# First norm by scale and transpose, decay matrices from running sums by transfer, and a refitted schedule table in a hybrid RG-LRU / DeltaNet layer

## Chip, cores and metric

One core of a Trainium2 chip runs the whole program. The metric is the device time of one execution in microseconds (us); three runs of the kernel before took 1097.16, 1097.39 and 1097.98 us, so the median is 1097.39 us.

## What is computed

One encoder layer on 512 tokens of 1024 features, all in float32: a norm, one wide projection, two token mixers side by side, a gated merge, a second norm and a SwiGLU. Cut to what matters here:

```
h = rmsnorm(x, mix_norm);  p = h @ w_in                      # 512 x 9248
y_rnn = rglru_branch(...)  @ w_rnn_proj                      # sigmoid, tanh, exp, sqrt, gelu; scans in both directions
y_dn  = deltanet_branch(...) @ w_dn_proj                     # 8 heads, both directions
x = x + (sig(g1) * y_rnn + sig(g2) * y_dn) @ w_out
x = x + (silu(h2 @ wg) * (h2 @ wu)) @ w_down;  h2 = rmsnorm(x);  out = rmsnorm(x)
# inside deltanet_branch, per head, direction and chunk:
gc = cumsum(g);  decay[i, j] = exp(gc[i] - gc[j]) where i >= j, else 0
A = strict_lower((beta k) k^T * decay);  att = q k^T * decay;  solve (I + A) ...;  state passes from chunk to chunk
```

The decay matrix is what one edit of the change computes in another way. The kernel uses chunks of 128 tokens, so there are 4 chunks (`NT`), 8 heads and 2 directions: 64 decay blocks of 128x128, held as 16 tiles of 128x512.

## The kernel before

**Products.** Nearly all matmuls are made of fp32r parts: a float32 operand is cast to fp32r (`whi`, `hh`: a CAST on ACT) and the rest is kept as a second part (`wlo`, `hl`: a subtraction on DVE), and three products of the parts are added up in PSUM. So each weight block of 128 columns costs a transfer on SP's queue (`wraw`), a CAST of 128x1024 on ACT, a subtraction of 128x1024 on DVE and 24 matmuls with 512 moving columns on PE. `whi` and `wlo` have two buffers each, `wraw` three.

**Stages.** (1) The first norm: each 128-token chunk of x is loaded, its squares are summed (ACT for even chunks, DVE for odd ones), and `norm_transpose` (L490) brings it to feature-major form; it multiplies each 128x128 block of x by `dg`, a diagonal matrix of 1/rms, so one float32 matmul scales and transposes at once. (2) The RG-LRU branch in four groups of three blocks (`rg_front`, `rg_mid`, `rg_out`): projections, four gate products per block, then Sigmoid, Tanh, Exp, Sqrt and Gelu on ACT, which need different function tables (each change is one ACT_TABLE_LOAD), and scans on DVE. (3) The DeltaNet branch in four groups of two heads: `dn_front` (projections, SiLU, norms), `dn_mats` (L813: decay, A and att, written to the tile `na`), `dn_inverse`, `dn_state`, `dn_out`. Projections of other stages fill PE in between. (4) Output projection, second norm, then the feed-forward part, in which PE never pauses.

**The decay before.** For each head and direction `dn_mats` builds on DVE two fp32r tiles of 128x512, a triangular mask (`upi` or `loi`) times the high and the low part of g (`gh`, `gl`); two matmuls with a strict triangular matrix (`slr` or `sur`) add these up to gc[i] - gc[j] in PSUM (`pd`); ACT takes one Exp of 128x512; then GpSimd (POOL) sets the masked half to zero with `affine_select`. The products with k and q follow on DVE (`na`).

**The order of the work.** Every operation is recorded by `Rec` (L322), all with the same source line, L374. `Plan.order` (L147) then plays the program through on estimated costs and due times, and the instructions are issued in the order that comes out. A due time is an entry of the table `TIMES` (L36), one per call of `spend()`, plus an offset within the stage; entries past the table's end follow its largest. Each engine takes the ready operation that is due first; a tile is handed out only when its pool has room. So the table sets the order on every engine, and each engine's queue is then in order: an instruction that waits holds back all that stand behind it on its engine.

Of the kernel before, what the change touches and what calls it, by code (L numbers as in the profile page):

```python
# [32 lines left out]
RELEASE = 200  # L33
SLACK = {"ACT": 1.1, "DVE": 1.1, "POOL": 1.2}
LOOK = 40
TIMES = [  # L36
# [18 lines left out]
class Plan:  # L55

# [5 lines left out]
    LAG = {("PE", "PE"): 0, ("PE", "DVE"): 250, ("PE", "ACT"): 250, ("DVE", "PE"): 320, ("ACT", "PE"): 320, ("POOL", "PE"): 320,  # L62
           ("DVE", "DVE"): 130, ("DVE", "ACT"): 250, ("ACT", "ACT"): 50, ("ACT", "DVE"): 200, ("DVE", "POOL"): 250,
           ("POOL", "DVE"): 150, ("ACT", "POOL"): 250, ("SP", "SP"): 0}

    def __init__(self, nc):
        self.nc = nc
        self.ops = []
        self.where, self.bases = [], []
        self.t = self.base = 0.0  # L70
# [7 lines left out]
        self.fixed = 13.3  # L78
# [40 lines left out]
    def add(self, eng, fn, outs, ins, cost, tail=0.0, table=None):  # L119
# [22 lines left out]
        cost *= SLACK.get(eng, 1.0)  # L142
        self.ops.append((eng, fn, deps, touched, round(cost), round(1.25 * tail), table, self.t))
# [3 lines left out]
    def order(self):  # L147
# [13 lines left out]
        for i, o in enumerate(ops):  # L161
            for d in o[2]:
                users[d].append(i)
        uses, first, last = {}, {}, {}
# [7 lines left out]
        need = [sorted((x for x in o[3] if x in self.tile_tag), key=first.get) for o in ops]  # L172
        free = dict(self.tags)
        queue = {tag: [] for tag in self.tags}
        for name, key in first.items():
            queue[self.tile_tag[name]].append((key, name))
# [9 lines left out]
        pe_end, cold = 0, WARM  # L186
        result, start = [], {}

        def slots(i):
            want = [x for x in need[i] if x not in held]  # L190
            taken = {}
            for name in want:
# [8 lines left out]
                for key, other in queue[tag]:  # L201
# [38 lines left out]
        while True:  # L240
            for e in ENGINES:
# [7 lines left out]
                for name in want:  # L249
                    tag = self.tile_tag[name]  # L250
                    free[tag] -= 1
                    held.add(name)
                    inuse[tag].add(name)
                    queue[tag].remove((first[name], name))
                c = o[4]
                if e == "ACT" and o[6] is not None and table not in o[6]:
                    table = o[6][0]
                    c += 1283
                if e == "PE":
                    if now - pe_end > 3000:  # L260
                        cold = 0
                    if cold < WARM:
                        c *= 2
                        cold += c
                    pe_end = now + c
                end = done = now + c
# [18 lines left out]
            while events and events[0][0] == now:  # L285
                _, kind, i = heapq.heappop(events)
                o = ops[i]
                if kind == 0:
                    busy[o[0]] = False
                elif kind == 1:  # L290
# [4 lines left out]
                    for u in users[i]:  # L295
                        left[u] -= 1
                        if not left[u]:
                            wait = 0 if o[5] else self.LAG.get((o[0], ops[u][0]), 200)
# [23 lines left out]
class Rec:  # L322
# [5 lines left out]
    def __getattr__(self, op):  # L328
        real = getattr(self.real, op)

        def call(*a, **kw):
# [9 lines left out]
            table, tail = None, 0.0  # L341
            e = self.eng
            if op == "dma_start":
                tail = max(out.nbytes() / 360.0, 1)
                cost = 450 if e == "SP" else 1000 if e == "POOL" else 60
            elif e == "PE":
                rhs = a[2] if op == "matmul" else a[1]
                n = elems(out)
                four_ = rhs.dtype == F32
                cols = elems(a[1]) if op == "matmul" else P  # L350
                if op == "transpose" and self.plan.fixed > 3:
                    cost = 110
                elif four_:
                    cost = 33 if cols == 32 else 81 if cols == 64 else n * 4 / 2.4
                else:
                    cost = max(n / 2.4, 107 if rhs.dtype == F32R else 54) + (self.plan.fixed if rhs.dtype == F32R else 2.5)
            elif e == "ACT":
                cost = (51 if psum else 93) + 0.834 * n + 93 * (ptr if n > 1 else len(ins) - 1) + (93 if len(outs) > 1 else 0)
                if op == "activation":
                    table = Plan.TABLES.get(a[2])  # L360
            elif e == "DVE":
                if op == "reciprocal":
                    cost = 69 + 6.25 * n
                elif op in ("tensor_tensor", "tensor_tensor_scan"):
                    cost = 69 + 1.042 * n
                elif op == "scalar_tensor_tensor":
                    cost = 130 + 1.042 * n + (70 if len(outs) > 1 else 0)
                elif op == "transpose":
                    cost = 68 + 1.042 * n
                else:  # L370
                    cost = 68 + (1.042 if psum else 0.521) * n + 61 * ptr
            else:
                cost = {"tensor_tensor": 150 + 2.1 * n, "memset": 35 + 0.834 * n, "affine_select": 140 + 0.886 * n}.get(op, 240 + 0.84 * n)
            self.plan.add(e, lambda: real(*a, **kw), outs, ins, cost, tail, table)  # L374
# [5 lines left out]
def trunk(ctx: ExitStack, tc: tile.TileContext, x, mix_norm, w_in, rg_conv_w, rg_conv_b, rg_wa, rg_ba, rg_wx, rg_bx,  # L380
# [15 lines left out]
    ps = ctx.enter_context(tc.tile_pool(name="ps", bufs=3, space=PSUM))  # L396

# [51 lines left out]
    slr, sur = (const([P, P], n, F32R) for n in ("slr", "sur"))  # L449
# [9 lines left out]
    V.tensor_copy(slr, sl)  # L459
    V.tensor_copy(sur, su)  # L460
# [29 lines left out]
    def norm_transpose(srcs, dgs, gain_, hh, hl, c0):  # L490
# [14 lines left out]
    xs = []  # L505
    for c in range(NT):
        xc = four(shape=(P, D))
        Q.dma_start(xc, x[0, c * P:(c + 1) * P, :])
        xs.append(xc)
        if c == 1:  # L510
            plan.t = -20.0
    plan.t = -300.0
    gain = load_gain(mix_norm[0], "gain1")
    hh = new(hp, (P, KD, S), "hh", 1, F32R)
    hl = new(hp, (P, KD, S), "hl", 1, F32R)
    for c0 in (0, 2):
        norm_transpose(xs[c0:c0 + 2], [norm_scale(xs[c0 + i], i) for i in range(2)], gain, hh, hl, c0)
        plan.t = -15.0
    plan.t = 0.0
# [147 lines left out]
    gh, gl = const([P, 64], "gh", F32R), const([P, 64], "gl", F32R)  # L667
    V.tensor_copy(gh, gt)
    V.tensor_tensor(gl, gt, f(gh), ALU.subtract)
# [7 lines left out]
    egc, elast, egl = ge[:, 0, :], ge[:, 1, :], ge[:, 2, :]  # L677
    negc = const([P, 64], "negc")
# [773 lines left out]
```

## Time and profile before

| | |
|---|---|
| median of three runs | 1097.39 us (1097.16 to 1097.98) |
| span of the profiled execution, first to last instruction | 1095.2 us |
| between that span and the median | 2.2 us |
| PE busy | 1070.3 us, 6916 records |
| DVE busy | 826.6 us |
| ACT busy | 626.6 us, 77.0 of it table loads |
| POOL busy | 46.1 us |
| moved by DMA | 98.40 MB, 90 GB/s on average |

The time of the profiled execution itself is not recorded beside its span; the 2.2 us is what the median of the runs has above it. PE is the matmul engine; PEld, its weight loads, runs beside it. A busy figure counts an instruction from its start to its end; matmuls overlap, so a row's mean is longer than the time from one start to the next. "Idle before <- releaser" is the time that the engine stood still ahead of a group and who ended that. Since nearly all work has the line L374, groups are told apart by tiles: `t` is any work tile of the two general pools, `mm`, `ax` and `st` are PSUM banks.

### The profile page before, as it was taken

To read this page: it belongs to the slowest core of one execution; us is meant where nothing else is said; L and a number is where in the kernel's file an instruction comes from. 1 tells how busy PE (TensorE), PEld (TensorE's weight loads), DVE (VectorE), ACT (ScalarE), POOL (GpSimd) and SP (SyncE) were. 2 spreads that over 40 slices of the span, in tenths; PEclk is the share of its full clock that TensorE was granted. 3 is DMA by queue.
4 is the path that set the end of the run, shared out by engine and by line. 5 is a ranking of instruction groups with operands and counts; after the bars stand their busy time and mean duration, and the time that the engine had idled before them with its cause. 6 is when DMAs were issued, how large, how long until landed. Compare 5 with 4: busy or idle time off the path is not lost.

```text
span 1095.2 us, 17616 instructions
## 1 busy us (share of the span) xinstructions
PE 1070.3 (98%) x6916; PEld 933.7 (85%) x6916; DVE 826.6 (75%) x1489; ACT 626.6 (57%) x1127; POOL 46.1 (4%) x93
## 2 busy tenths in 40 slices
PE   7999899999999999999999999999999999999997
PEld 6988678888887878788798888789999999988886
DVE  6686999669994798589759847868898988872432
ACT  6779997797346653766575254446544444451223
POOL 2000000002020010020000000000000000000000
PEclk9999999999999999999999999999999999999999
DMA  7342313232322033104211313441233334332332
GB/s 196 103 116 67 88 55 104 82 92 72 101 82 67 8 111 103 53 20 113 80 35 45 96 49 121 135 140 58 78 116 108 98 104 116 102 111 96 97 97 77
DMA packets 160787, 98.40 MB, mean 90 GB/s; under 512 B 4800, under 2 KB 151344, under 8 KB 160704
## 3 DMA queue, kind: packets, MB, share of 16 engines
q1 hardware_dynamic: 159232, 93.99, 29.6%
q10 hardware_dynamic: 1184, 3.15, 0.8%
q8 instruction: 54, 0.88, 0.3%
q14 instruction: 29, 0.24, 0.1%
q0 software_dynamic: 288, 0.13, 0.0%
HBM read 95.17 MB, written 2.10 MB: 89 GB/s over the span
## 4 chain that ended last, share of the span: by engine, by line
PE 87%; DVE 7%; ACT 4%; issue 1%; DMA 1%; SPq 0%; DVEq 0%
PE mm L374 50%; PE ax L374 22%; PE st L374 15%; DVE t L374 5%; ACT t L374 2%; DVE wlo L374 1%; ACT na L374 1%; DMA wraw<-in_w_in_dram 1%; DVE na L374 1%; ACT whi L374 1%; ACT L374 0%; DVE hl L374 0%; ACT ax L374 0%; SPq L374 0%; ACT hh L374 0%
## 5 line engine op out<-in xcount | busy, mean ns | idle before, releaser
L374 ACT CAST whi<-wraw 128x1024 fp32r<-128x1024 f32 (+2 forms) x150 | 146.6, 978 | 206.8 <-PE mm L374 83.2
L374 DVE TENSOR_TENSOR wlo<-wraw,whi 128x1024 fp32r<-128x1024 f32 (+2 forms) x149 | 168.8, 1135 | 122.3 <-ACT whi L374 75.0
L374 PE MATMUL mm<-hh,whi 128*128 128x512 f32 (+2 forms) x704 | 242.4, 356 | 3.7 <-ACT whi L374 3.6
L374 PE MATMUL mm<-hl,whi 128*128 128x512 f32 (+2 forms) x704 | 241.9, 356 | 0.0
L374 DVE TENSOR_TENSOR t<-t,t 128x512 fp32r<-128x512 f32 (+16 forms) x414 | 212.4, 524 | 17.0 <-ACT t L374 10.4
L374 PE MATMUL mm<-hh,wlo 128*128 128x512 f32 (+1 forms) x688 | 155.6, 356 | 0.0
L374 PEld LDWEIGHTS mm<-hh,whi 128*128 128x128 f32 (+1 forms) x704 | 133.0, 189 | 22.2 <-ACT whi L374 5.0
L374 PEld LDWEIGHTS mm<-hl,whi 128*128 128x128 f32 (+1 forms) x704 | 133.0, 189 | 16.9
L374 PEld LDWEIGHTS mm<-hh,wlo 128*128 128x128 f32 x688 | 115.9, 189 | 16.9
L374 DVE SCALAR_TENSOR_TENSOR t<-mm,par,t 128x511 f32<-128x511 f32 (+1 forms) x108 | 80.0, 743 | 21.0 <-ACT t L374 20.3
L374 PE MATMUL ax<-t,t 32*32 32x32 f32 (+3 forms) x876 | 90.9, 263 | 1.8 <-issue 0.8
L374 PE MATMUL mm<-t,whi 128*128 128x512 f32 x320 | 83.0, 397 | 0.6 <-DVE t L374 0.4
L374 ACT CAST t<-t 128x512 fp32r<-128x512 f32 (+1 forms) x95 | 64.7, 687 | 32.3 <-DVE t L374 29.0
L374 PEld LDWEIGHTS ax<-t,t 128*128 128x128 f32 (+1 forms) x876 | 74.2, 153 | 10.3 <-ACT t L374 2.9
L374 ACT ACT_TABLE_LOAD x60 | 77.0, 1283 | 6.4 <-PEq L1438 1.7
L374 PEld LDWEIGHTS mm<-t,whi 128*128 128x128 f32 x320 | 59.0, 188 | 14.5 <-ACT whi L374 1.9
L374 PE MATMUL mm<-t,t 128*128 128x256 f32 (+1 forms) x372 | 66.4, 322 | 0.0
L374 PEld LDWEIGHTS mm<-t,t 128*128 128x128 f32 x372 | 54.8, 191 | 4.9
L374 ACT ACTIVATE t<-t 128x128 f32<-128x128 f32 (+4 forms) x84 | 45.8, 558 | 13.0 <-DVE t L374 9.5
L374 PE MATMUL mm<-t,wlo 128*128 128x512 f32 x160 | 43.0, 393 | 0.5 <-DVE wlo L374 0.5
L374 PE MATMUL st<-hh,whi 128*128 128x512 f32 (+1 forms) x112 | 42.1, 380 | 0.3 <-ACT whi L374 0.3
L374 PE MATMUL st<-hl,whi 128*128 128x512 f32 (+1 forms) x112 | 41.7, 377 | 0.0
(219 smaller groups left out, 1808.0 us busy)
## 6 DMA issues: line engine op xcount, KB each, us to landing
wraw<-in_w_in_dram SPq DMA_DIRECT2D x72, 512.0 KB, 3.8
wraw<-in_w_gate_up_dram SPq DMA_DIRECT2D x44, 512.0 KB, 3.9
wraw<-in_w_down_dram SPq DMA_DIRECT2D x22, 512.0 KB, 3.7
wraw<-in_w_rnn_proj_dram SPq DMA_DIRECT2D x16, 384.0 KB, 3.6
wraw<-in_w_out_dram SPq DMA_DIRECT2D x8, 512.0 KB, 4.7
wraw<-in_w_dn_proj_dram SPq DMA_DIRECT2D x8, 384.0 KB, 3.5
t<-in_x_dram SPq DMA_DIRECT2D x4, 512.0 KB, 5.3
na<-in_x_dram ACTq DMA_DIRECT2D x4, 512.0 KB, 7.5
```

Source lines behind the costliest of these rows:

```text
L374: self.plan.add(e, lambda: real(*a, **kw), outs, ins, cost, tail, table)
```

## The change

Three edits go together.

1. **First norm.** `norm_scale` now multiplies the chunk itself by 1/rms, the first half of the features on DVE, the second on ACT, and `norm_transpose` uses plain transposes against the identity in place of the float32 matmuls against `dg`. The chunks are loaded in pairs, and each pair is a stage of its own (`spend()`).
2. **Decay.** The running sums gc, which a small product had already put into PSUM (`pg`), are copied to `gcs`, negated (`ngc`), transposed once, and written to memory (`gsum`, 64x128, a transfer on ACT's queue). For each head and direction, one transfer on SP's queue repeats a row of 512 sums over all 128 partitions, `affine_select` puts -1e30 into the masked half, and four Exps of 128x128 with the bias `-gc[j]` give the decay. The masks' fp32r copies, `gh`, `gl`, the 32 DVE products and the 32 matmuls go.
3. **Planner.** Costs are stated as time occupied and latency, with new numbers; `RELEASE` goes from 200 to 60; a change between small-tile and full-tile matmuls costs `TURN`; a PE operation may follow another as soon as PE is free; and `TIMES` is replaced by a longer table of other numbers, which now also covers the feed-forward part.

The diff, cut to what the prediction speaks of:

```diff
-RELEASE = 200
-SLACK = {"ACT": 1.1, "DVE": 1.1, "POOL": 1.2}
+RELEASE = 60
+TURN = 115
 TIMES = [
-    -6353, -2179, -3830, -1814, 8399, -797, -1690, -2060, -5604, -305, -389, 556, 449, 4234, 332, -1074, 274, 462,
...
+    -8668, -8998, -7367, -8122, -4337, -4464, -3716, -1005, -2335, -2489, -4826, -54, 780, -1893, -464, 5564, -585,
...
+                    if self.modes[i] != mode:
+                        mode = self.modes[i]
+                        c += TURN
+                        l += TURN
...
     def norm_scale(src, c):
-        dg = small([P, P], "dg", 4)
-        V.tensor_scalar(dg, ident, rms_rstd(src, c), None, ALU.mult)
-        return dg
+        rin = rms_rstd(src, c)
+        sc = four(shape=(P, D))
+        V.tensor_scalar(sc[:, 0:512], src[:, 0:512], rin, None, ALU.mult)
+        A.activation(sc[:, 512:D], src[:, 512:D], AF.Copy, scale=rin)
+        return sc
...
-                    T.matmul(pt[:, (2 * j + i) * P:(2 * j + i + 1) * P], srcs[i][:, kt * P:(kt + 1) * P], dgs[i], start=True, stop=True)
+                    turn(pt[:, (2 * j + i) * P:(2 * j + i + 1) * P], srcs[i][:, kt * P:(kt + 1) * P])
...
+    gcs, ngc = const([P, 64], "gcs"), const([P, 64], "ngc")
+    V.tensor_copy(gcs, pg[:, 0:64])
+    V.tensor_scalar(ngc, gcs, -1.0, None, ALU.mult)
+    pgt = axb()
+    turn(pgt[0:64, 0:P], gcs)
+    gts = const([64, P], "gts")
+    A.copy(gts, pgt[0:64, 0:P])
+    gsum = dp.tile([64, P], F32, name="gsum")
+    plan.keep.add(gsum.tensor.name)
+    A.dma_start(gsum, gts)
+    grow = gsum.rearrange("(d r) t -> d (r t)", d=2)
...
                 c0 = 32 * d + 4 * h
-                rh, rl = two(F32R), two(F32R)
-                mk = (upi if d == 0 else loi).unsqueeze(1).to_broadcast([P, NT, P])
-                for r_, g_ in ((rh, gh), (rl, gl)):
-                    V.tensor_tensor(r_.rearrange("p (c i) -> p c i", c=NT), mk, f(g_[:, c0:c0 + 4]).unsqueeze(2).to_broadcast([P, NT, P]), ALU.mult)
-                pd = axb()
-                lt = slr if d == 0 else sur
-                T.matmul(pd, lt, rh, start=True, stop=False)
-                T.matmul(pd, lt, rl, start=False, stop=True)
                 dt_ = two()
-                act(dt_, pd, AF.Exp)
                 dv = dt_.rearrange("p (c i) -> p c i", c=NT)
-                G.affine_select(out=dv, in_=dv, pattern=[[0, NT], [1 - 2 * d, P]], compare_op=ALU.is_ge, fill=0.0, base=0,
+                Q.dma_start(dt_, grow[d, S * h:S * (h + 1)].partition_broadcast(P))
+                G.affine_select(out=dv, in_=dv, pattern=[[0, NT], [1 - 2 * d, P]], compare_op=ALU.is_ge, fill=-1e30, base=0,
                                 channel_multiplier=2 * d - 1)
+                for c in range(NT):
+                    act(dv[:, c, :], dv[:, c, :], AF.Exp, bias=ngc[:, c0 + c:c0 + c + 1])
                 dts.append(dt_)
```

The new table moves instructions on every engine. Three places are shown, with buffer numbers after the names (L374 of before is L405 of after).

**Start, PE.** `dg` are the diagonal matrices, `t` with `ident` a transpose, `hh` and `hl` the parts of the normed x, `whi` a weight part. Before, the products with the second pair of chunks begin behind the first pair's last block:

```order
L374 MATMUL ax_111<-dg_98,t_89 128x128
L374 MATMUL ax_111<-dg_103,t_90 128x128
L374 MATMUL ax_122<-dg_112,t_91 128x128
L374 MATMUL ax_123<-dg_112,t_91 128x128
L374 MATMUL mm_134<-hh_96,whi_133 64x256
L374 MATMUL mm_134<-hl_97,whi_133 64x256
L374 MATMUL ax_122<-dg_117,t_92 128x128
```

Now, at the same place on PE, the first projection of the RG-LRU branch (`mm_177`) runs on the first 256 tokens, and the second pair's transposes come after it:

```order
L405 MATMUL ax_109<-ident_81,t_100 128x128
L405 MATMUL ax_109<-ident_81,t_105 128x128
L405 MATMUL mm_177<-hh_89,whi_175 128x256
L405 MATMUL mm_177<-hl_90,whi_175 128x256
```

So a full weight block's product has moved ahead of the second half of the norm, and the small product `mm_134` behind it.

**Second group of the RG-LRU branch, ACT.** Tanh has the factor `rgt`, Exp the factor `rgs`; `whi` is a weight cast that PE needs next. Before, a load of the Exp table and two Exps stand between two casts, and the second cast follows one that reads DVE's result (`t_274`):

```order
L374 CAST whi_322<-wraw_321 128x1024
L374 CAST t_466<-graw_465 128x512
L374 ACTIVATE t_281<-t_220,rgt_153 128x512 x2
L374 ACT_TABLE_LOAD
L374 ACTIVATE t_220<-t_220,rgs_152 128x512 x2
L374 CAST t_274<-t_269 128x512
L374 CAST whi_292<-wraw_291 128x1024
L374 ACTIVATE t_282<-t_235,rgt_153 128x512 x2
L374 ACTIVATE t_235<-t_235,rgs_152 128x512
L374 CAST t_268<-t_263 128x512
```

Now the group's six Exps stand in one block behind one load, ahead of the next two casts:

```order
L405 CAST whi_295<-wraw_294 128x1024
L405 ACTIVATE t_308<-ax_319,par_127 128x512
L405 ACTIVATE t_286<-t_253,rgt_153 128x512
L405 ACTIVATE t_359<-mm_387,zero_t_129,par_127 128x512
L405 ACT_TABLE_LOAD
L405 ACTIVATE t_223<-t_223,rgs_152 128x512 x2
L405 ACTIVATE t_238<-t_238,rgs_152 128x512 x2
L405 ACTIVATE t_253<-t_253,rgs_152 128x512 x2
L405 ACT_TABLE_LOAD
L405 ACTIVATE t_284<-t_284 128x1024
L405 CAST whi_325<-wraw_324 128x1024
```

The Exps have been drawn together, and more work stands between two weight casts there.

**First group of the DeltaNet branch, ACT.** Before, the first decay tile (`t_556`) takes one Exp behind one load, between weight casts:

```order
L374 CAST whi_378<-wraw_377 128x1024
L374 ACTIVATE t_442<-mm_449,par_127 128x512
L374 ACT_TABLE_LOAD
L374 ACTIVATE t_556<-ax_555 128x512
L374 CAST whi_462<-wraw_461 128x1024
```

Now the first decay tile (`t_552`) has four Exps with the bias `ngc`, and loads for SiLU, Gelu and Sqrt stand between them:

```order
L405 ACT_TABLE_LOAD
L405 ACTIVATE t_552<-t_552,ngc_157 128x128
L405 ACT_TABLE_LOAD
L405 ACTIVATE t_481<-st_482 128x512
L405 ACTIVATE t_359<-mm_374,zero_t_129,par_127 128x512
L405 CAST whi_412<-wraw_411 128x768
L405 ACT_TABLE_LOAD
L405 ACTIVATE t_552<-t_552,ngc_157 128x128
L405 CAST whi_344<-wraw_343 128x1024
L405 ACTIVATE t_552<-t_552,ngc_157 128x128
L405 ACT_TABLE_LOAD
```

One tile's Exps are spread over several loads. Over the whole program ACT's table loads go from 60 to 71, PE's matmuls from 6127 to 6096, and DVE loses the 32 products of 128x512.

More of the change, by code (lines that the diff above doesn't have):

```diff
@@ L117, in region, with add @@
         return name, p0, p0 + dims[0][1], mask
-    def add(self, eng, fn, outs, ins, cost, tail=0.0, table=None):
+    def add(self, eng, fn, outs, ins, occ, lat, tail=0.0, table=None, mode=0):
         i = len(self.ops)
@@ L163, in order @@
                 users[d].append(i)
+        number = {name: i for i, name in enumerate(self.tile_tag)}
         uses, first, last = {}, {}, {}
@@ L171, in order @@
                     last[name] = max(last.get(name, key), key)
-        need = [sorted((x for x in o[3] if x in self.tile_tag), key=first.get) for o in ops]
+        need = [sorted((x for x in o[3] if x in self.tile_tag), key=lambda x: (first[x], number[x])) for o in ops]
         free = dict(self.tags)
@@ L200, in slots @@
                 moves, ups = [], 0
-                for key, other in queue[tag]:
+                for key, _, other in queue[tag]:
                     if other == name:
@@ L253, in order @@
                     inuse[tag].add(name)
-                    queue[tag].remove((first[name], name))
-                c = o[4]
+                    queue[tag].remove((first[name], number[name], name))
+                c, l = o[4], o[7]
                 if e == "ACT" and o[6] is not None and table not in o[6]:
@@ L265, in order @@
                     pe_end = now + c
-                end = done = now + c
+                end, done = now + c, now + l
                 if o[5]:
@@ L289, in order @@
                     busy[o[0]] = False
+                    if o[0] == "PE":
+                        for u in users[i]:
+                            if ops[u][0] == "PE":
+                                left[u] -= 1
+                                if not left[u]:
+                                    insort(ready["PE"], (when[u], u))
                 elif kind == 1:
@@ L344, in call @@
                 tail = max(out.nbytes() / 360.0, 1)
-                cost = 450 if e == "SP" else 1000 if e == "POOL" else 60
+                occ = 450 if e == "SP" else 1000 if e == "POOL" else 66
             elif e == "PE":
                 rhs = a[2] if op == "matmul" else a[1]
[L348 to L354, printed above, removed]
-                else:
-                    cost = max(n / 2.4, 107 if rhs.dtype == F32R else 54) + (self.plan.fixed if rhs.dtype == F32R else 2.5)
+                n, cols = elems(out), elems(a[1]) if op == "matmul" else P
+                if op == "transpose":
+                    occ = 109
+                elif rhs.dtype == F32R:
+                    occ = 120 if n <= 256 else n / 2.4 + 13.5
+                elif cols < P and kw.get("tile_position") is not None:
+                    mode, occ = 1, 17 if cols == 32 else 58
+                else:
+                    occ = max(223, 2 * (2 * n / 2.4 + 2))
+                lat = occ + 163
             elif e == "ACT":
-                cost = (51 if psum else 93) + 0.834 * n + 93 * (ptr if n > 1 else len(ins) - 1) + (93 if len(outs) > 1 else 0)
+                src = ins[0].space == PSUM if ins else False
+                occ = (64 + 0.82 * n if src else 90 + 0.845 * n) + 95 * ptr
+                if len(outs) > 1:
+                    occ += 115 if src else 95
+                lat = occ + 100
                 if op == "activation":
@@ L516, in trunk @@
     for c0 in (0, 2):
-        norm_transpose(xs[c0:c0 + 2], [norm_scale(xs[c0 + i], i) for i in range(2)], gain, hh, hl, c0)
-        plan.t = -15.0
-    plan.t = 0.0
+        xs = []
+        for c in (c0, c0 + 1):
+            xc = four(shape=(P, D))
+            Q.dma_start(xc, x[0, c * P:(c + 1) * P, :])
+            xs.append(xc)
+        if c0 == 0:
+            gain = load_gain(mix_norm[0], "gain1")
+        norm_transpose([norm_scale(xs[i], i) for i in range(2)], gain, hh, hl, c0)
+        spend()
     prow = two(shape=(P, 2, P))
```

64 lines of the change are left out of this document (29 added, 35 removed), and 25 rows, old and new, of the table TIMES.

## Prediction

> **What bounds the kernel now.** First the page: busy time of each engine, and the engines' shares of the chain of work that ended last.
>
> ```profile
> span 1095.2 us, 17616 instructions
> PE 1070.3 (98%) x6916; PEld 933.7 (85%) x6916; DVE 826.6 (75%) x1489; ACT 626.6 (57%) x1127; POOL 46.1 (4%) x93
> PE 87%; DVE 7%; ACT 4%; issue 1%; DMA 1%; SPq 0%; DVEq 0%
> ```
>
> PE is the bound: 98% busy and 87% of the chain. A change gains what it takes from PE's own work and from PE's pauses. Where those pauses lie is told by the busy time of each engine in seven stretches; the columns are the stretch, its length, busy time with count of PE, its weight loads, DVE, ACT and POOL, then PE's granted clock, the DMA engines' share and GB/s.
>
> ```profile
> 0.00:25.00 25.00, 17.67 (x113) 15.99 (x114) 15.35 (x40) 16.90 (x36) 6.65 (x21) 1.00 0.76 202
> 25.00:100.00 75.00, 75.00 (x427) 66.02 (x426) 52.84 (x80) 62.35 (x88) 0.61 (x2) 1.00 0.35 99
> 100.00:125.00 25.00, 21.36 (x86) 16.87 (x85) 21.44 (x24) 20.96 (x28) 0.00 (x0) 0.93 0.19 53
> 125.00:300.00 175.00, 174.54 (x777) 142.72 (x775) 153.53 (x213) 131.97 (x199) 9.34 (x18) 1.00 0.31 88
> 300.00:700.00 400.00, 392.75 (x2847) 328.61 (x2846) 306.65 (x684) 219.23 (x482) 29.51 (x52) 1.00 0.25 71
> 700.00:1050.00 350.00, 350.00 (x2465) 329.74 (x2464) 262.55 (x429) 160.50 (x273) 0.00 (x0) 1.00 0.35 106
> 1050.00:1095.20 45.20, 38.95 (x212) 33.72 (x211) 14.26 (x24) 14.70 (x25) 0.00 (x0) 0.95 0.25 83
> ```
>
> From 700 to 1050 PE never pauses: a shorter path ahead of that stretch shifts it as a whole. PE idles 25.00 − 17.67 = 7.33 us at the start, 45.20 − 38.95 = 6.25 at the end, and 3.64 + 0.46 + 7.25 = 11.35 between 25 and 1050. ACT has 25 − 16.90 + 75 − 62.35 + 25 − 20.96 = 24.8 us free in the first 125 us, 43 in the next 175, and 181 from 300 to 700.
>
> Then PE's waits by releaser (in total, times, longest), and the timeline around the largest one past the start (start, length, instruction).
>
> ```profile
> PE ax L374 <- DVE dg L374: 3.9, 2, 3.6
> PE mm L374 <- ACT whi L374: 3.6, 2, 2.5
> ...
> 112.11 1.34 ACT L374 ACTIVATE t<-t,rgt 128x512 f32<-128x512 f32 x2
> 113.47 1.28 ACT L374 ACT_TABLE_LOAD   x1
> 114.76 1.34 ACT L374 ACTIVATE t<-t,rgs 128x512 f32<-128x512 f32 x2
> 115.31 0.39 PE L374 MATMUL mm<-hl,whi 128*128 128x512 f32 x1
> 117.13 1.04 ACT L374 CAST whi<-wraw 128x1024 fp32r<-128x1024 f32 x1
> 118.22 0.79 PE L374 MATMUL mm<-hh,whi 128*128 128x512 f32 x1 [2.52 <-ACT whi L374]
> 118.81 0.63 PE L374 MATMUL mm<-hl,whi 128*128 128x512 f32 x1
> ...
> 121.37 0.50 PE L374 MATMUL mm<-hl,whi 128*128 128x512 f32 x1
> ```
>
> ACT is in order: the weight cast that PE needs stands behind a table load, two pairs of activations, and one cast that waits for DVE. So ACT, though 57% busy over the span, is what stops PE here.
>
> **The change part by part.** The sum starts from 1095.2 us of span plus the 2.2 by which the median, 1097.4, lies above it; I take that 2.2 as unchanged.
>
> *Decay products.* Two groups of 16 matmuls go; the third row, from the chain of work (start, length), gives a matmul's pitch.
>
> ```profile
> L374 PE MATMUL ax<-t,slr x16: 387/393/585, 109.8 to 494.1; 128*128 128x512 f32 x16
> L374 PE MATMUL ax<-t,sur x16: 387/394/577, 110.2 to 496.8; 128*128 128x512 f32 x16
> ...
> 1072.37 12.27 PE mm L374 x54
> ```
>
> A row lasts 0.39, but 54 queued ones end in 12.27 us: 0.227 each. 32 × 0.227 = 7.3 us off PE's work, all on the path: **−7.3**. If the place that each pair leaves is taken by a wait, nothing is gained: bounds −7.3 and 0.
>
> *First norm.* 32 float32 matmuls appear as 64 records, and 32 transposes take their place. Rows: the first blocks and a later run of the same kind, the group as a whole, and transposes of this kernel.
>
> ```profile
> 8.68 4.02 PE L374 MATMUL ax<-dg,t 128*128 128x128 f32 x18 [0.34 <-DVE dg L374]
> 12.86 1.39 PE L374 MATMUL ax<-dg,t 128*128 128x128 f32 x10 [0.15 <-DVE hl L374]
> ...
> L374 PE MATMUL ax<-dg,t 128*128 128x128 f32 x64 | 11.2, 335 | 4.4 <-DVE dg L374 3.9 <-DVE rin L374 0.4 <-DVE hl L374 0.2
> L374 PE MATMUL ax<-ident,t 128*128 128x128 f32 x162 | 24.2, 273 | 0.8 <-ACT ax L374 0.8
> L374 ACT ACTIVATE t<-t 128x1024 f32<-128x1024 f32 x22 | 22.8, 1055 | 1.5 <-DMA t<-in_x_dram 1.4
> L374 ACT ACTIVATE t<-t,rgt 128x512 f32<-128x512 f32 x24 | 15.7, 717 | 0.0
> ```
>
> Early records pass at 4.02/18 = 0.22 us, later ones at 0.14. Sixteen gone at 0.22 and sixteen at some 0.11 (an estimate between 0.14 and half of 0.22) is 5.3 us at most. Against it: half a chunk is now scaled on ACT, 0.72 (the 128x512 with a factor) and behind the next chunk's squares, 1.06: 1.8 us later. Further, the first 256 tokens' projection now runs before the second pair, so that pair's wait (most of the 3.9 for `dg`) gets cover. Bounds −5.3 and +1.8 (nothing saved, as PE waits for chunks there anyway). I take **−2**, nearer the middle, since the delay can eat most of the saving.
>
> *PE's pauses by the new order.* From 115.31 to 118.22 is 2.91 us from start to start, 2.68 more than the pitch of 0.227, where the row shows 2.52: each row understates by about 0.16. Then the clock: the window shows 0.93, and after this pause seven matmuls take 121.37 − 118.22 = 3.15 us where seven pitches are 1.59, another 1.6 us. With 14 such waits shown in the timeline, the pauses between 25 and 1050 cost 11.35 + 14 × 0.16 + 1.6 = 15 us. In the new order the second group's six Exps stand in one block behind one load, and table loads there no longer cut between the casts one by one; full weight blocks fill the gaps of the small products. I take four fifths recovered, **−12**; bounds 0 and −15. That is my choice, and the largest uncertain term.
>
> The Trainium skill ("TensorE: Matmul & The Clock Gate", section "Part 1: The HAM clock gate") says that PE falls back to half clock only after a whole idle window of some 3.4 us. By that a 2.5 us pause would cost 2.7 and this term, by estimate, come out near −11, the sum near 1077; the trace disagrees, with slow matmuls after 2.9 us, and the measurement decides.
>
> *DVE.* Four groups of eight products of 128x512 go.
>
> ```profile
> L374 DVE TENSOR_TENSOR t<-loi,gh 128x512 fp32r<-128x512 f32 x8 | 5.9, 742 | 1.1 <-PE ax L374 1.1
> L374 DVE TENSOR_TENSOR t<-upi,gh 128x512 fp32r<-128x512 f32 x8 | 5.9, 741 | 0.0
> L374 DVE TENSOR_TENSOR t<-upi,gl 128x512 fp32r<-128x512 f32 x8 | 5.6, 701 | 0.2 <-PE ax L374 0.2
> L374 DVE TENSOR_TENSOR t<-loi,gl 128x512 fp32r<-128x512 f32 x8 | 5.5, 687 | 3.5 <-ACT t L374 3.5
> ```
>
> 5.9 + 5.9 + 5.6 + 5.5 = 22.9 us, off the path (DVE has 93 us free from 300 to 700): **0** by itself; it helps the pauses above.
>
> *ACT.* It gains 11 table loads and 64 Exps of 128x128 with a bias, and gives up 16 Exps of 128x512.
>
> ```profile
> L374 ACT ACT_TABLE_LOAD x60 | 77.0, 1283 | 6.4 <-PEq L1438 1.7 <-PE ax L374 1.5 <-DVE so L374 1.3
> L374 ACT ACTIVATE t<-ax,par 128x512 f32<-128x512 f32 x48 | 30.5, 688 | 7.2 <-PE ax L374 6.8
> L374 ACT ACTIVATE t<-ax 128x512 f32<-128x512 f32 x20 | 12.0, 598 | 8.4 <-PE ax L374 8.2
> L374 ACT ACTIVATE t<-t 128x128 f32<-128x128 f32 x32 | 9.6, 302 | 7.8 <-DVE t L374 6.3 <-PE ax L374 1.5
> ```
>
> Loads: 11 × 1.283 = 14.1 us. Exps: a 128x128 takes 0.302, and a per-partition operand costs up to 0.688 − 0.598 = 0.09 more, so 64 × 0.30 to 0.39 = 19 to 25, less 16 × 0.598 = 9.6. The norm's halves: 4 × 0.717 = 2.9. In all 26 to 32 us more. What hides it is ACT's free time, 43 us from 125 to 300 and 181 to 700: **0**. But group 0's decay stands where ACT had 4 us free of 25 (100 to 125), and what doesn't fit there lands on PE through the weight casts: 0 to +32 as bounds, the gone cover is the slower rival below.
>
> The Trainium skill ("ScalarE: Activation LUTs", section "What ACT_TABLE_LOAD costs") puts a change of tables at 1283 ns plus a drain of some 1380, and says to batch work by table. By that estimate 11 more loads cost 29.3 us of ACT, not 14.1, and with half of it ahead of PE's casts the kernel would be slower. The load's length agrees with the row; the 6.4 us idle ahead of all 60, 0.1 each, shows no such drain.
>
> *DMA.* Sixteen reads of 256 KB on SP's queue join its weight loads, and one write of 32 KB on ACT's. POOL keeps its 16 selects, now ahead of the Exp. The nearest row is a write of that size (issue to landing 2.2 us):
>
> ```profile
> out_dram<-t ACTq DMA_DIRECT2D x4, 256.0 KB, 2.2
> ```
>
> The DMA engines are 0.19 to 0.31 busy from 100 to 700, and each transfer needs only the sums, known long before; a transfer that waits for a free tile holds back the weight loads behind it on SP. **0**, at worst 16 × 2.2 = 35 us.
>
> *End.* The last 512-wide product now stands next to the end, before the narrower ones: at most one 512-wide row against one 256-wide more in the last chain, 0 to +0.6 by the pitches above: **0**.
>
> Sum: −7.3 − 2 − 12 = −21.3, so 1097.4 − 21.3 = **1076**.
>
> **The rivals.** *B, the pauses only move:* PE's work shrinks by 7.3 + 2 and other casts come late in place of the old ones: 1097.4 − 9.3 = 1088. For it: the change puts more on ACT, which is the releaser now. Against: the waits' largest places are rebuilt.
>
> *C, the pauses go altogether:* with the full 15 of pauses, the full 5.3 of the norm, and the first wait of 3.6 covered, −7.3 − 15 − 5.3 − 3.6 = −31, 1066. For it: from 700 on PE shows that it can run without a pause; against, small products depend on each other through DVE and ACT.
>
> *D, slower: ACT becomes PE's releaser in the first 200 us.* Half of the new loads, 5.5 × 1.28 = 7 us, and 16 new Exps, 5 to 6 us, in a stage where ACT had 24.8 us free in 125, delay the casts of `whi` one for one; `whi` has two buffers only, so ACT can run little ahead. The price of 13 on B's 1088 is 1101. It decides, above no change, once more than 9 us of ACT's 26 to 32 fall on PE. For it: spread Exps, one tile behind three loads; against: ACT's free 43 and 181 us right after.
>
> *E, the decay comes late:* sums go to memory and back, the transfers stand behind weight loads in SP's queue, and the products with k wait; the gains are given back, 1096 to 1097. Against: the first transfer needs only sums computed early, and projections can fill.
>
> **How the numbers follow.** Chances: the forecast 0.50 (1069 to 1083: from a third of the pauses recovered to all of them with 4 more from the norm or the start), B 0.21, C 0.14, D 0.10, E 0.05. The range from 1063 to 1090 holds the forecast, B and C, and leaves D and E out. 0.2% is 2.2 us, about what a measurement of this kernel can tell from no change: the forecast, B and C are faster, 0.85; E the same, 0.05; D slower, 0.10.
>
> **What would show it.** Right: PE's busy time near 1060, no rows with `slr` and `sur`, DVE near 804, ACT near 655 with 71 loads; the window 100 to 125 at clock 1.00 with PE idle under 1 us; 16 transfers of 256 KB landing in 2 to 3 us with nobody waiting for them. B: the pauses between 25 and 1050 still near 11 us, on other releasers. D: PE waits for `whi` from ACT before 200 us, of over 9 us in total. E: PE or DVE waiting for POOL or DMA tiles of the decay. Wrong in the norm's step: the first matmul of a projection later than before, or the second pair's transposes waited for.

## The result and the profile after

The kernel after takes 1089.0 us (median of 4 runs, 1088.5 to 1089.1) against 1097.7 of the kernel before: a ratio of 0.9919, 95% interval 0.9907 to 0.9931, 8.7 us faster where 21 were forecast. The page of the kernel after, the lines that answer to those of before:

```profile
span 1086.6 us, 17571 instructions
PE 1064.3 (98%) x6853; PEld 922.4 (85%) x6853; DVE 813.0 (75%) x1455; ACT 652.1 (60%) x1191; POOL 44.0 (4%) x93
```

The same stretches as before (the columns as there), then PE's largest waits:

```profile
0.00:25.00 25.00, 15.94 (x98) 14.29 (x99) 15.51 (x38) 18.75 (x38) 6.64 (x21) 1.00 0.75 203
25.00:100.00 75.00, 73.93 (x405) 62.68 (x404) 55.03 (x78) 66.15 (x95) 0.00 (x0) 1.00 0.35 95
100.00:125.00 25.00, 25.00 (x111) 20.38 (x110) 24.93 (x31) 24.88 (x34) 0.00 (x0) 1.00 0.39 105
125.00:300.00 175.00, 174.25 (x773) 142.00 (x772) 148.12 (x205) 148.13 (x242) 19.43 (x29) 1.00 0.36 102
300.00:700.00 400.00, 395.61 (x2852) 330.41 (x2851) 302.43 (x671) 223.77 (x497) 17.90 (x43) 1.00 0.28 80
700.00:1050.00 350.00, 349.21 (x2458) 326.56 (x2457) 253.86 (x414) 157.09 (x266) 0.00 (x0) 1.00 0.33 99
1050.00:1086.60 36.60, 30.40 (x167) 26.11 (x166) 13.13 (x23) 13.37 (x24) 0.00 (x0) 0.98 0.26 87
...
PE ax L405 <- DVE t L405: 5.9, 4, 3.9
PE ax L405 <- DVE ident L405: 2.6, 1, 2.6
PE ax L405 <- ACT t L405: 2.3, 5, 0.7
PE ax L405 <- DVE gcs L405: 1.1, 1, 1.1
```

Of the 8.6 us that the span lost, 6.0 are busy time of PE. Its idle time between 25 and 1050 fell from 11.35 us to 1.07 + 0 + 0.75 + 4.39 + 0.79 = 7.00; the stretch from 100 to 125, where the largest pause stood, has none now, and its clock is 1.00. At the start PE idles 9.06 us in place of 7.33, and two pauses are new: 1.1 us for `gcs`, whose transpose stands in PE's queue ahead of other work, and 0.79 in the feed-forward part. The added work is what the prediction counted, 71 table loads and 64 Exps; three sizes are off: the transfers land in 3.5 us where 2 to 3 were forecast, DVE's busy time is 813.0 where 804 was, and PE's is 1064.3 where 1060 was.

```profile
L405 ACT ACT_TABLE_LOAD x71 | 91.1, 1283 | 4.3 <-PEq L1468 1.7 <-DVE so L405 1.4 <-DMA t<-gsum 0.2
L405 ACT ACTIVATE t<-t,ngc 128x128 f32<-128x128 f32 x64 | 21.3, 394 | 0.2
...
t<-gsum SPq DMA_DIRECT2D x16, 256.0 KB, 3.5
```

### The profile page after: what moved, and what is told of

The parts are those of the page before. It is cut to its first block, busy times and chain, and to the rows that moved or that the text cites. A ratio compares the mean times of both kernels' runs of the same rounds, so it can differ in the third digit from the quotient of the medians.

```text
span 1086.6 us, 17571 instructions
## 1 busy us (share of the span) xinstructions
PE 1064.3 (98%) x6853; PEld 922.4 (85%) x6853; DVE 813.0 (75%) x1455; ACT 652.1 (60%) x1191; POOL 44.0 (4%) x93
## 4 chain that ended last, share of the span: by engine, by line
PE 81%; DVE 10%; ACT 7%; issue 1%; DMA 1%; DVEq 0%; ACTq 0%
PE mm L405 44%; PE ax L405 22%; PE st L405 15%; DVE t L405 7%; ACT t L405 3%; DVE wlo L405 2%; ACT na L405 1%; ACT whi L405 1%; ACT L405 1%; DVE na L405 1%; DMA wraw<-in_w_down_dram 0%; DMA t<-in_x_dram 0%; ACT rst L405 0%; ACT hh L405 0%; DVE rin L405 0%
## 5 line engine op out<-in xcount | busy, mean ns | idle before, releaser
L405 ACT CAST whi<-wraw 128x1024 fp32r<-128x1024 f32 (+2 forms) x150 | 145.8, 976 | 194.5 <-PE mm L405 87.3
L405 DVE TENSOR_TENSOR t<-t,t 128x512 fp32r<-128x512 f32 (+16 forms) x414 | 213.3, 524 | 40.9 <-ACT t L405 33.2
L405 PE MATMUL mm<-hh,whi 128*128 128x512 f32 (+2 forms) x704 | 242.9, 357 | 0.7 <-ACT whi L405 0.7
L405 DVE TENSOR_TENSOR wlo<-wraw,whi 128x1024 fp32r<-128x1024 f32 (+2 forms) x149 | 169.4, 1139 | 99.2 <-ACT whi L405 94.4
L405 PE MATMUL mm<-hl,whi 128*128 128x512 f32 (+2 forms) x704 | 242.2, 356 | 0.0
L405 PE MATMUL mm<-hh,wlo 128*128 128x512 f32 (+1 forms) x688 | 155.8, 356 | 0.0
L405 PEld LDWEIGHTS mm<-hh,whi 128*128 128x128 f32 (+1 forms) x704 | 133.1, 189 | 18.3 <-ACT whi L405 1.3
L405 PEld LDWEIGHTS mm<-hl,whi 128*128 128x128 f32 (+1 forms) x704 | 133.1, 189 | 17.3 <-DVE hl L405 0.2
L405 PEld LDWEIGHTS mm<-hh,wlo 128*128 128x128 f32 x688 | 116.3, 189 | 16.6
L405 ACT CAST t<-t 128x512 fp32r<-128x512 f32 (+1 forms) x95 | 64.6, 688 | 64.8 <-DVE t L405 58.1
L405 PE MATMUL ax<-t,t 32*32 32x32 f32 (+3 forms) x876 | 93.0, 264 | 3.1 <-ACT t L405 2.2
L405 PEld LDWEIGHTS ax<-t,t 128*128 128x128 f32 (+1 forms) x876 | 74.3, 153 | 13.6 <-ACT t L405 6.1
L405 DVE SCALAR_TENSOR_TENSOR t<-mm,par,t 128x511 f32<-128x511 f32 (+1 forms) x108 | 80.2, 743 | 4.4 <-ACT t L405 3.6
L405 PE MATMUL mm<-t,whi 128*128 128x512 f32 x320 | 82.8, 396 | 0.3 <-DVE t L405 0.3
L405 PEld LDWEIGHTS mm<-t,whi 128*128 128x128 f32 x320 | 58.7, 188 | 14.0 <-DVE t L405 1.1
L405 PE MATMUL mm<-t,t 128*128 128x256 f32 (+1 forms) x372 | 66.7, 322 | 0.0
L405 ACT ACTIVATE t<-t 128x128 f32<-128x128 f32 (+4 forms) x84 | 46.0, 556 | 23.1 <-DVE t L405 20.3
L405 PEld LDWEIGHTS mm<-t,t 128*128 128x128 f32 x372 | 54.6, 190 | 5.2 <-DVE na L405 0.2
L405 PE MATMUL st<-hh,whi 128*128 128x512 f32 (+1 forms) x112 | 42.2, 379 | 0.4 <-ACT whi L405 0.4
L405 PE MATMUL mm<-t,wlo 128*128 128x512 f32 x160 | 42.5, 392 | 0.0
L405 PE MATMUL st<-hl,whi 128*128 128x512 f32 (+1 forms) x112 | 41.9, 377 | 0.0
```

The source lines that it names most:

```text
L405: self.plan.add(e, lambda: real(*a, **kw), outs, ins, occ, lat, tail, table, mode)
```

## Experiments

Theory: the gain is small because the pauses that the prediction wanted to recover come from the order as a whole and were only partly recovered, and because the norm's saved matmuls were not on the path. Rivals: ACT's added work, or the transfers, ate it. Ratios are against the kernel before, from the same chip.

### One edit at a time, planned anew

Three kernels are the kernel before with the decay edit, the norm edit or both, old planner and old table; the fourth is the kernel after with the old norm.

```diff
 decay_only, decay_norm_old_plan, in dn_mats of the kernel before:
-                act(dt_, pd, AF.Exp)
+                Q.dma_start(dt_, grow[d, S * h:S * (h + 1)].partition_broadcast(P))
...
+                    act(dv[:, c, :], dv[:, c, :], AF.Exp, bias=ngc[:, c0 + c:c0 + c + 1])
 norm_only, decay_norm_old_plan: norm_scale and norm_transpose as after, loops as before
 new_plan_old_norm, in norm_scale of the kernel after:
-        sc = four(shape=(P, D))
+        dg = small([P, P], "dg", 4)
+        V.tensor_scalar(dg, ident, rms_rstd(src, c), None, ALU.mult)
```

> The kernel before with the decay edit alone; planner, table of due times and norm as before. Theory 1 (each edit brings its own PE work, the order the rest): 32 matmuls x 0.227 = 7.3 us less than the kernel before, so about 1090, with PE's pauses between 25 and 1050 us near the 11.35 of before. Theory 2 (the order is what counts): the old table was made for other operations, the pauses grow and eat the saving: 1095 to 1100, pauses of 18 us and more.

> The kernel before with the norm edit alone (scale, then transpose), in the loop order of before; planner, table and decay as before. Theory 1, the prediction's term: 2 us less, about 1095.5. Theory 2 (the start belongs to the chunks and the clock, not to PE's count of matmuls): the half as many matmuls leave PE idle between chunks, it stays at half clock longer, and nothing is gained: 1097 to 1099, first full-rate matmul no earlier than the 12.4 us or so of before.

> The kernel before with both edits of the work, decay and norm, and the old planner and table. Theory 1: 1097.5 - 7.3 - 2 = 1088, so the new planner and table add next to nothing to what the kernel after shows (1089.0). Theory 2: 1095 to 1100, so that the new table is what makes the two edits pay, by 6 to 11 us.

> The kernel after with the norm of before (diagonal matrices, float32 matmuls), all else as after. Theory 1, the prediction's term: 2 us slower than after, about 1091. Theory 2 (clock): the doubled matmuls keep PE busy and bring the clock up sooner, so the time is the same as after or less, 1086 to 1089.

Measured: decay_only 1109.7 (ratio 1.0109, 1.0096 to 1.0123), norm_only 1106.1 (1.0074, 1.0061 to 1.0088), decay_norm_old_plan 1113.4 (1.0141, 1.0128 to 1.0155), new_plan_old_norm 1097.6 (1.0002, 0.9994 to 1.0011). Each edit alone makes the kernel slower by 8 to 12 us, and taking the norm edit out of the kernel after costs 8.6. None of the four falls into a range that its theories gave: each came out slower, the first three by 7 to 13 us above the upper end of theory 2, so planning anew on the old table cost far more than that theory had it. Theory clock of the fourth falls. Where the time goes in decay_only: its page, two stretches, its largest waits, and its timeline.

```profile
PE 1063.2 (96%) x6885; PEld 928.9 (84%) x6885; DVE 812.8 (73%) x1455; ACT 645.3 (58%) x1182; POOL 45.5 (4%) x93
...
100.00:125.00 25.00, 13.20 (x52) 10.52 (x51) 18.46 (x20) 19.71 (x27) 0.00 (x0) 0.77 0.08 22
125.00:200.00 75.00, 67.36 (x284) 54.73 (x283) 65.76 (x75) 60.74 (x81) 3.34 (x5) 0.94 0.29 81
...
PE mm L374 <- ACT whi L374: 13.2, 4, 11.8
PE st L374 <- ACT whi L374: 7.4, 1, 7.4
...
115.82 1.33 ACT L374 ACTIVATE t<-t,rgs 128x512 f32<-128x512 f32 x2
120.28 0.62 ACT L374 CAST t<-t 128x512 fp32r<-128x512 f32 x1 [3.12 <-DVE t L374]
120.80 1.04 ACT L374 CAST whi<-wraw 128x1024 fp32r<-128x1024 f32 x1
...
121.89 0.80 PE L374 MATMUL mm<-hh,whi 128*128 128x512 f32 x1 [11.80 <-ACT whi L374]
```

PE's own work fell by 7.1 us, as forecast, but PE stood still for 11.8 us. ACT was not busy all that time: it was itself idle for 3.12 us, waiting for DVE, with the cast of `whi` behind that wait. In the kernel before, a cast stands ahead of this work, and the next is the one at 117.13 that the prediction shows:

```profile
110.65 1.03 ACT L374 CAST whi<-wraw 128x1024 fp32r<-128x1024 f32 x1
```

None of the decay's instructions is there (the first nine of its Exps stand at 91 to 96 us, the next at 185). The planner had put the cast further back. In new_plan_old_norm the time goes far from the edit: at 300 us it is about level with the kernel after, but PE is busy 6.9 us less from 300 to 500, with waits of up to 2.8 us for `whi` and for tiles of DVE. First new_plan_old_norm, then the kernel after:

```profile
300.00:500.00 200.00, 190.27 (x1376) 158.45 (x1375) 149.99 (x348) 115.37 (x269) 12.91 (x31) 0.97 0.26 73
```

```profile
300.00:500.00 200.00, 197.14 (x1428) 165.17 (x1427) 158.59 (x363) 117.53 (x273) 13.70 (x31) 1.00 0.28 76
```

So these four times don't tell what an edit is worth: each also changes the order everywhere.

### The edits at a fixed order

Four kernels issue every instruction that is not of the edit in a recorded order, that of before for the first three, that of after for the last:

```diff
-        todo = plan.order()
+        todo = []
+        for a, n in zip(ORDER[0::2], ORDER[1::2]):
+            todo += range(a, a + n)
```

> The kernel before with the decay edit, but without planning anew: every other instruction is issued in the order of the kernel before, written out as a list; a tile's four Exps stand where its one Exp stood, its transfer and select some 8 and 3 us of planned time ahead. Theory order (what the planned-anew kernel with the decay edit lost came from where the planner put other instructions): PE's work falls by 7.3 us and the pauses stay as before, so about 1090 to 1091. Theory ACT (64 Exps are 10 us more of ACT than 16, and that delays the weight casts): 1097 or more, with new waits of PE for casts near 110, 260, 305 and 475 us. Theory transfers (sums through memory are late): POOL or ACT waits for the transfers end in waits of PE.

> The kernel before with the norm edit, all other instructions in the order of the kernel before; the half chunk on ACT stands right beside DVE's half. Theory clock: transposes pass as slowly as before while PE is at half clock, PE waits for chunks and comes up to full clock later; the first projection of 512 columns starts no earlier than the 22.2 us of before: 1097 to 1099. The prediction's term: 1095.5. Theory order: whatever the 8 us of the planned-anew kernel with this edit were, they are not in the start; past 25 us PE's pauses are those of before.

> Both edits of the work in the order of the kernel before. Theory order: 1090 to 1092, the sum of the two runs with one edit; then the new planner and table bring 1 to 3 us on top of that to the kernel after (1089.0). The prediction's terms without any gain of the order: 1088.

> The kernel after with the norm of before (diagonal matrices, float32 matmuls) and every other instruction in the order of the kernel after. Theory order: the 8.6 us that the planned-anew kernel with this norm lost lie in the order; here it is within 1.5 us of after, 1088 to 1090.5, or faster, since PE is kept busy and comes to full clock sooner. The prediction's term: 2 us slower than after, 1091.

Measured: fixed_decay 1093.6 (0.9964, 0.9952 to 0.9977), 4.2 us faster; fixed_norm 1097.5 (1.0000, 0.9991 to 1.0009); fixed_both 1094.7 (0.9974, 0.9963 to 0.9984), 3.1 us faster; fixed_after_dg 1089.7 (0.9930, 0.9917 to 0.9942), the kernel after within 0.7 us. The swings of 8 to 16 us are gone: they were the order's. The norm edit shows no gain in either order, and the decay brings 4.2 of its 7.3. Theory order missed two times all the same: fixed_decay lies between its theories and fixed_both above theory order, since PE's idle time between 25 and 1050 didn't stay at 11.35 us but came to 15.88 in fixed_decay. The 1.1 us between fixed_decay and fixed_both are inside their intervals. From both edits in the old order to the kernel after, the order brings 1094.7 − 1089.0 = 5.7 us.

### What became of the decay's other 3 us, and of ACT's added work

Two kernels have one Exp of 128x512 per decay tile, without the bias, so the decay they compute is another; one is in the order of before, one in that of after. The table experiment keeps the new costs and puts the old due times under them.

```diff
 fixed_decay_one (on fixed_decay), one_exp (on the kernel after):
-                for c in range(NT):
-                    act(dv[:, c, :], dv[:, c, :], AF.Exp, bias=ngc[:, c0 + c:c0 + c + 1])
+                act(dt_, dt_, AF.Exp)
 new_costs_old_table (on the kernel after): TIMES of before behind
+    -6353, -6353,
```

> The kernel before with the decay edit in the order of before, but one Exp of 128x512 without bias in place of each tile's four; it leaves out the subtraction of the column's sum. Theory ACT (the four Exps cost 3 of the 7 us in an order that was not made for them): 1090 to 1091.5. Rival (transfers, selects or lost matmuls elsewhere): 1093 to 1094, as with four.

> The kernel after in its own order, with one Exp of 128x512 without bias in place of the four of 128x128 with bias for each decay tile; it leaves out the subtraction of the column's sum, so the decay it computes is another. ACT has some 10 to 13 us less to do. Theory cover (ACT's added work is hidden where the order was made for it): 1088.5 to 1089.5, as after. Rival (ACT's packed first 200 us set PE's pace): 2 to 6 us faster, 1083 to 1087, with the gain ahead of 200 us.

> The kernel after (both edits of the work, new planner costs) with the table of the kernel before, its first entry repeated for the two stages that the norm's pairs add. Theory table (the due times fitted to this set of instructions are what takes the 24 us back that the old plan with both edits loses): 1100 to 1115. Rival (the new costs and rules by themselves give the planner a true picture, and any table will do): 1089 to 1095.

Measured: fixed_decay_one 1091.0 (0.9945, 0.9932 to 0.9959); one_exp 1088.5 (0.9921, 0.9908 to 0.9934); new_costs_old_table 1104.0 (1.0059, 1.0047 to 1.0071). Busy time of fixed_decay and then of fixed_decay_one from 300 to 700 us:

```profile
300.00:700.00 400.00, 390.42 (x2836) 326.53 (x2835) 299.12 (x672) 227.40 (x521) 21.95 (x52) 1.00 0.29 81
```

```profile
300.00:700.00 400.00, 392.81 (x2850) 329.11 (x2849) 302.10 (x676) 222.16 (x487) 21.68 (x52) 1.00 0.30 82
```

With one Exp, PE gets back 2.4 us there, all of it between 400 and 500 us, where 28 of the 64 Exps stand. In the old order ACT's longer chain so took 2.1 us by the ratios, 2.6 by the medians and by PE's idle time (the two intervals overlap a little, so the size is not sharp); the transfers, the same in both kernels, did not. Table loads have no part in it: fixed_decay has 60 like the kernel before, so the 11 further loads of the kernel after came with the new order and not with the edit. What is left of PE's added idle time lies mostly from 100 to 125, where PE idles 5.4 us in both kernels in place of 3.64: in the kernel before, decay matmuls stand there ahead of a wait of 1.12 us for a cast, and without them the wait is 1.80. In the order of after the same cut, 15 us of ACT's busy time (652.1 to 637.2, four table loads among it), moves the time by 0.6 us, within the intervals: there the added work is hidden, as the prediction had it. With the old table the new costs lose 15 us to the kernel after, the larger part again by a late cast in the stretch from 100 to 125 (10.0 us of wait for `whi`):

```profile
100.00:125.00 25.00, 15.00 (x58) 11.96 (x58) 19.96 (x21) 20.34 (x28) 0.00 (x0) 0.82 0.08 21
...
PE mm L396 <- ACT whi L396: 10.9, 3, 10.0
```

### The start: clock or chain

The timeline of PE at the start of the kernel after: transposes pass at 2.18/9 = 0.24 us, and the first products with 256 columns at 0.21 each, until 16.4 us.

```profile
6.70 0.90 PE L405 MATMUL ax<-ident,t 128*128 128x128 f32 x3 [3.87 <-DVE t L405]
8.89 2.18 PE L405 MATMUL ax<-ident,t 128*128 128x128 f32 x9 [1.28 <-DVE t L405]
11.72 1.09 PE L405 MATMUL ax<-ident,t 128*128 128x128 f32 x4 [0.65 <-DVE hl L405]
13.48 0.58 PE L405 MATMUL mm<-hh,whi 128*128 128x256 f32 x1 [0.67 <-ACT whi L405]
13.86 0.41 PE L405 MATMUL mm<-hl,whi 128*128 128x256 f32 x1
14.07 0.41 PE L405 MATMUL mm<-hh,whi 128*128 128x256 f32 x1
...
16.42 0.69 PE L405 MATMUL ax<-ident,t 128*128 128x128 f32 x3
```

Extra matmuls keep PE busy there, in the order of after (warm_start), of before (before_warm), of before with the norm edit (norm_warm), and together with the cut table (warm_flat); ffn_flat has the cut table alone.

```diff
             gain = load_gain(mix_norm[0], "gain1")
+            spare = stb()
+            for i in range(17):
+                T.matmul(spare[:, 0:P], ident, ident, start=True, stop=True)
 ffn_flat, warm_flat: TIMES[158:] left out
```

> The kernel after, every instruction in its order, with 17 float32 matmuls more that multiply the identity by itself into a spare PSUM bank: 8 while PE waits for the first chunk, the others in the pauses between the first transposes. Theory clock (the norm edit saves no time since PE, with half the matmuls, stays at half clock longer): the 256-column products that run at 0.21 us from 13.5 to 16.2 in the kernel after run at 0.12, and PE is 1 to 2 us ahead at 25 us: 1087 to 1088. Rival (the chunks' own chain sets the start, not the clock): the time stays within 0.5 us of 1089.0, or is later by the dummies that don't fit a pause.

> The kernel before, in its own order, with 8 float32 matmuls more of the identity by itself while PE waits for the first chunk (its later run of products with the diagonal matrices has no pause to fill). Theory clock: full clock before 8 us in place of some 12.5, 0.5 to 2 us faster than before, 1095.5 to 1097. Rival (chunks' chain): unchanged, 1097.5.

> The kernel before with the norm edit in the order of before, and 19 such matmuls more, 8 ahead of the first chunk and 11 in the pauses between the first transposes. Theory clock alone (the norm edit saves PE 2 us once the clock is the same): 2 us below the kernel before with the 8 extra matmuls, 1093.5 to 1095. Rival (the longer chain scale, transpose, copy eats it, whatever the clock): not below that kernel, 1095.5 to 1097.5.

> The kernel after with its table of due times cut to the first 158 entries, so that the feed-forward part follows the largest of them, as in the kernel before; the order is the same up to some 670 us. Theory tail (the new table's entries for the feed-forward part bring pauses that the kernel before doesn't have: 2.5 us of PE time between 950 and 1050): 1086 to 1087.5, no pause past 700 us. Rival (these entries pay): 1089 or more.

> The kernel after with the table cut to 158 entries, and the 17 extra matmuls at the start. If the two losses are independent: 1089.0 - 2.5 - 1.1 = 1085.4. If the start's gain is taken up by the feed-forward pauses or the other way round: 1086.4 or more.

Measured: warm_start 1086.5 (0.9899, 0.9886 to 0.9911), before_warm 1097.8 (1.0001, 0.9992 to 1.0009), norm_warm 1098.0 (1.0005, 0.9996 to 1.0014), ffn_flat 1087.9 (0.9916, 0.9900 to 0.9932), warm_flat 1086.8 (0.9904, 0.9891 to 0.9918). PE's start in warm_start, then in before_warm:

```profile
3.04 3.78 PE L834 MATMUL st<-ident 128*128 128x128 f32 x16
...
7.24 1.06 PE L834 MATMUL st<-ident 128*128 128x128 f32 x8
8.97 1.49 PE L834 MATMUL ax<-ident,t 128*128 128x128 f32 x9 [0.68 <-DVE t L834]
13.38 0.39 PE L834 MATMUL mm<-hh,whi 128*128 128x256 f32 x1 [0.46 <-ACT whi L834]
13.60 0.28 PE L834 MATMUL mm<-hl,whi 128*128 128x256 f32 x1
13.72 0.28 PE L834 MATMUL mm<-hh,whi 128*128 128x256 f32 x1
...
15.04 0.66 PE L834 MATMUL ax<-ident,t 128*128 128x128 f32 x3
```

```profile
8.59 2.27 PE L793 MATMUL ax<-dg,t 128*128 128x128 f32 x18 [1.05 <-DVE dg L793]
12.82 1.39 PE L793 MATMUL ax<-dg,t 128*128 128x128 f32 x10 [1.96 <-DVE hl L793]
```

Last, the first product with 512 columns in before_warm and in norm_warm, and two of the products with 256 columns in fixed_after_dg:

```profile
22.05 0.39 PE L793 MATMUL mm<-hh,whi 128*128 128x512 f32 x1
...
23.15 0.40 PE L794 MATMUL mm<-hh,whi 128*128 128x512 f32 x1
...
14.32 0.28 PE L833 MATMUL mm<-hl,whi 128*128 128x256 f32 x1
14.44 0.28 PE L833 MATMUL mm<-hh,whi 128*128 128x256 f32 x1
```

In the order of after the clock matters: a whole weight block runs on the first 256 tokens there, and at full clock PE comes to the second pair's transposes at 15.04 in place of 16.42. The norm of before, in the same order, brings these products to 0.12 us each as well (fixed_after_dg): PE has 32 passes for the first pair there in place of 16, and the products that follow run at full pace. The kernel with the extra matmuls takes 2.5 us less than the kernel after by the medians (the intervals of the two ratios overlap by a little; the spans are 1085.0 and 1086.6). In the order of before the clock is worth nothing: the run of 18 takes 2.27 us in place of 4.02, and the next run begins at 12.82 in place of 12.86, because it waits for `hl` from DVE. At that clock the norm edit (norm_warm) still saves nothing, and its first product with 512 columns comes 1.1 us later: here theory clock fell, and the chain of each chunk (sum of squares, scale, transpose, copies) sets the start. The feed-forward pauses are gone from the trace of ffn_flat (350.00 of 350 us busy), but 1.1 us are inside its spread (1086.0 to 1092.6), and warm_flat is no faster than warm_start: what they cost is not settled. The lowest median is that of warm_start.

## Why the prediction was wrong

- **Decay products, −7.3, all on the path.** PE's work fell as forecast (7.1 us in decay_only). At a fixed order 4.2 us of time came of it. The prediction priced ACT's added work at zero because ACT had time free in the stretch as a whole; in the old order, in the places where a tile's Exps stand, PE gave 2.1 to 2.6 us back, which one Exp in place of four recovers. Part of the rest is the bound that the prediction named, "the place that each pair leaves is taken by a wait".
- **First norm, −2.** Measured 0 in the old order and at most about 1 us in the new, inside the intervals. It is the bound that the prediction named and set aside, "nothing saved, as PE waits for chunks there anyway". Its other half, that the projection of 256 tokens covers the second pair's wait, holds in the kernel after, but that projection then ran at half pace from 13.5 to 16.4 us, because the transposes keep PE less busy than the products with `dg` did. The prediction had no term for that. Its sign of being wrong, a first projection that starts later, shows in the old order only (15.55 us in fixed_norm, 15.03 before).
- **PE's pauses by the new order, −12.** This is the step that failed most. The largest pause went as described, and with it the slow matmuls (stretch 100 to 125, clock 0.93 to 1.00). But four fifths of all pauses was a choice, read from one place of the order, a wait for a weight cast. Idle time between 25 and 1050 fell by 4.35 us of 11.35; from 300 to 700, 4.39 of 7.25 are still there, and the start and the `gcs` transpose added some 2.8. The pauses from 300 to 700 are of another kind: none of PE's waits that the profile lists there ends on a cast of `whi`, in either kernel, and most are small products that wait for a tile of DVE or ACT. PE's largest waits in that stretch, before and then after:

```profile
PE ax L374 <- DVE t L374: 3.6, 5, 0.9
...
PE ax L405 <- ACT t L405: 2.3, 5, 0.7
PE ax L405 <- DVE t L405: 0.8, 2, 0.6
```

By the runs at fixed order the order brought 5.7 us. What would remove the waits that are left was not tested.

- **The sum.** −3.1 for both edits in the old order and −5.7 for the order make −8.8, measured −8.7; they add up by construction, since both steps meet at fixed_both. The time is nearly that of rival B (1088), but by luck, from another sum: not PE's full 9.3 with unchanged pauses, but a third of it and half of the pauses' term.
- **Rival D.** Late casts of `whi` did cost 10 to 14 us in one wait in decay_only, decay_norm_old_plan and new_costs_old_table, near 110 us, where and about as it was priced. Its cause was put wrongly: not ACT's amount of work, but where the cast stood in ACT's queue; with the same work in the recorded order the longest wait for `whi` is 3.0 us (fixed_decay). The new table avoids that in the kernel after.
- **Transfers, DVE, end.** No wait of PE in the kernel after ends on the transfers or on POOL, though POOL waits for them 124 us in all, so rival E did not come. DVE's products of 22.9 us went, but its busy time fell by 13.6 only, and no run shows what that did by itself.

## What to carry to other kernels

Where a planner sets the order, an edit's own worth is measured by replaying the recorded order around it; planned anew with a table that was fitted to other instructions, a good edit of 4 us read as a loss of 12 here. In decay_only, ACT was busy 58% of the span and still stopped PE for 11.8 us, because the cast that PE needed stood behind an instruction that waited; so read the queue at the pause and not the busy share. Before counting matmuls saved at a start, look whether PE had been waiting there for its inputs.

## What the runs showed of the hardware

- The granted clock of the profile reads 1.00 for the first 25 us of all these kernels, while the same products with 256 columns pass at 0.21 us in the kernel after and at 0.12 in warm_start: the half pace at the start is seen in the timeline only. In warm_start the pace doubled after some 4 us of unbroken matmuls (3.04 to 7.24).
- How long PE pauses doesn't settle by itself whether the matmuls behind the pause are slow. In fixed_decay PE waits 1.80 us for one cast and 2.99 us for the next, and the matmuls behind both run at full pace (rows of 0.39 us). In fixed_both it waits the same 1.80 us for the same cast, and seven of the matmuls that follow run at half pace (rows of 0.63). First fixed_decay, then fixed_both:

```profile
119.49 0.50 PE L789 MATMUL mm<-hh,whi 128*128 128x512 f32 x1 [2.99 <-ACT whi L789]
119.83 0.39 PE L789 MATMUL mm<-hl,whi 128*128 128x512 f32 x1
...
113.42 0.50 PE L789 MATMUL mm<-hh,whi 128*128 128x512 f32 x1 [1.80 <-ACT whi L789]
...
114.36 0.63 PE L789 MATMUL mm<-hl,whi 128*128 128x512 f32 x1
```

So the prediction's step from a pause of 2.9 us to slow matmuls holds for the trace of before, and no rule by length follows from it.

- The 64 Exps of 128x128 with a bias per partition have a mean row of 394 ns, the upper end of the price that was taken (0.30 to 0.39). The row of 302 ns that the lower end came from is no Exp: those 32 activations square a tile and add it up (`so`).
- In the kernel before, Tanh (`rgt`) runs behind Exp (`rgs`) with no table load between (the ACT order shown for the second group), so not every change among the five functions named there costs a load.
